# A two-layer recurrent trunk: beta and decay columns in fp32 strips, other order at the beginning, for low parts, state update and output factor

## The chip, the cores and the metric

The kernel runs on one core of a Trainium2 chip. The metric is the device time of one execution in microseconds (us), the median of several runs. The core's engines work side by side: TensorE (PE) multiplies matrices into PSUM, VectorE (DVE) and ScalarE (ACT) work elementwise, GpSimd (POOL) does small element work and issues some transfers, SyncE (SP) issues the weight transfers.

## What is computed

The reference is a decoder trunk of two layers over 256 prompt tokens and 8 x 8 sample tokens, 320 tokens in all, with a width of 1024. Each layer is a half-step feed-forward block (SwiGLU, 2816 wide), a mixer, and another half-step feed-forward block, each with an RMS norm before and after; a last norm follows. The mixer reads one input projection:

```python
proj = h @ w_in     # [rg_x | q | k | v | rg_gate | z | beta_logit | decay_logit]
conv_out, new_buf = causal_conv(proj[..., :CONV_CH], conv_buf, conv_w)   # width 4, on rg_x, q, k, v
beta = sigmoid(scal[..., :DN_HEADS])
g = -exp(dn_a_log) * softplus(scal[..., DN_HEADS:] + dn_dt_bias)
o, S = gated_delta(q, k, v, g, beta, S0)
o = rmsnorm(o, dn_norm_w) * silu(z)
```

One half of its width is a gated linear recurrence (`rg_lru`), the other a gated delta rule with four heads of 128, computed in chunks of 64 tokens with a triangular solve per chunk. Beta and decay are the last 8 of 3080 columns of `w_in`. The final states are outputs too.

## The kernel before

Activations are kept transposed, features on the partitions and 320 tokens along the free dimension. A product in fp32 accuracy is made of three fp32r products: a weight block of 128 columns is loaded by SP as `raw` (L122), ScalarE rounds it to its high part `wh` (L130), VectorE subtracts to get the low part `wl` (L135), and `Unit.mm` (L158) issues `xh*wh`, `xh*wl` and `xl*wh` for each of 8 blocks of the contraction, 24 matmuls a unit. There are five raw buffers, and three pairs for wh and wl beside two larger spare ones.

PE's order is written out by hand, the other engines' order is laid out by the compiler from priorities: `tc.high_priority(offset=n)` puts instructions ahead as if they had been written n places earlier. A `Fill` object holds a stage's units; `F(n)` issues the next n of their matmuls, `F.to(i)` all up to unit i, and the small matmuls of the mixer are put between such calls, so that the fills cover the waits of the small work. The lists FL, FZ and FY (L60) hold these n.

At the boundary to the mixer (`boundary`, L404) the residual is updated block by block, and `F.inter` issues three matmuls of each of the first four units for every block: the 8-column unit of beta and decay and the first three of k. Its PSUM tile is scaled in `scal_done` (L710), transposed at L760 into token order, and VectorE makes beta and g of it in a row of small operations (L765 to L773, softplus at L264 to L276). The units of k, q, v, rg, z and gate follow; each finished unit of the first four kinds goes through `conv` (L662: L674, L675, three L686, an activation at L707). g is summed by the matmuls from L796 on, decay differences are made at L828, k*k at L892, the solve runs from L914 on, and q*k at L936 needs all four q heads. The recurrence's gates (L1070) and scan (`rg_scan`, L1073) run beside it.

At the end, two blocks p of sample states are updated: four matmuls each (L1212, 32 rows by 512 columns), four additions into the state (L1216), two transfers out. `scale_o` (L1047) multiplies the outputs by a root factor, made on POOL by a power (L1052), and `finish_o` transposes them (L1225).

The program begins (L1296 on) with the loads of x and of the first three weight units in halves, dummy matmuls on a tile of ones (L1330), transposes of x (L1335, L1336), and the first 72 matmuls. Then come the sums of squares (L1412) and the first row factor rsb (L1421, L1422).

## Time and profile before

| | us |
|---|---|
| median of 3 runs (1279.4 to 1281.31) | 1279.9 |
| the profiled execution | 1281.22 |
| its span | 1279.3 |
| PE busy | 1250.1 |
| VectorE busy | 853.2 |
| ScalarE busy | 698.1 |
| GpSimd busy | 109.3 |

The span runs from the first to the last instruction; what the execution takes beyond it lies around it. PE busy is the union of its matmul durations, which overlap, so a busy PE need not be at its peak. The granted clock is TensorE's, 1.00 for full speed. Times in the rows count from the start of the span; the mixers of the two layers stand at about 256 to 395 and 880 to 1017 us.

### The profile page before, as it was taken

The page shows a single profiled execution, that of the slowest core. Times are in us where ns is not written, and L with a number is a line of the kernel's source. Part 1 is how long each engine was busy: PE and PEld are TensorE (multiplying, and loading weights), DVE is VectorE, ACT ScalarE, POOL GpSimd, SP SyncE. Part 2 cuts the span into 40 slices and gives each one's busy share as a digit, 9 for nine tenths or more (in the row PEclk, how much of TensorE's full clock was granted, in tenths as well). Part 3 has the DMA queues.
Part 4 walks back from the last instruction along what each step waited for, and adds up shares of the span by engine and source line. Part 5 has one row for each costly group of instructions (what it writes and reads, how often), then busy time and mean ns, then how long its engine had stood idle before and what let it go on. Part 6 is the DMA issues. An engine that isn't in the chain of part 4 may idle for free.

```text
span 1279.3 us, 24478 instructions
## 1 busy us (share of the span) xinstructions
PE 1250.1 (98%) x9812; PEld 1216.5 (95%) x9812; DVE 853.2 (67%) x1541; ACT 698.1 (55%) x1220; POOL 109.3 (9%) x241
## 2 busy tenths in 40 slices
PE   9999999998999999999999999999899999999996
PEld 7999999998979999999999999999899899999995
DVE  4976644799776866654486665459986877666444
ACT  5654444675686644444464444446749675444443
POOL 1100000232130100000000000013411210000000
PEclk9999999998989999999999999999999899999998
DMA  8555555563346455555645555575332655555551
GB/s 207 156 171 161 161 152 167 137 159 84 84 131 174 118 165 160 161 152 168 181 118 159 162 165 153 164 193 141 89 84 59 186 152 166 164 165 156 147 143 42
DMA packets 356470, 187.26 MB, mean 146 GB/s; under 512 B 9034, under 2 KB 353436, under 8 KB 356356
## 3 DMA queue, kind: packets, MB, share of 16 engines
q1 hardware_dynamic: 353124, 178.12, 49.3%
q0 software_dynamic: 2672, 6.65, 1.9%
q8 instruction: 77, 1.26, 0.4%
q10 hardware_dynamic: 560, 0.93, 0.2%
q14 instruction: 37, 0.30, 0.1%
HBM read 179.16 MB, written 6.51 MB: 145 GB/s over the span
## 4 chain that ended last, share of the span: by engine, by line
PE 90%; DVE 6%; ACT 2%; DMA 1%; issue 1%; POOL 0%; SPq 0%; DVEq 0%; ACTq 0%
PE mm L158 44%; PE sm L158 38%; PE sm L914 2%; PE st L231 1%; DMA raw<-in_ffn_w_up_dram 1%; PE sm L978 1%; DVE co L686 1%; DVE wl L135 1%; DVE xr L1094 1%; DVE aux L1216 0%; PE sm L936 0%; DVE nA L921 0%; DVE DN L828 0%; PE sm L1070 0%; DVE bt L425 0%
## 5 line engine op out<-in xcount | busy, mean ns | idle before, releaser
L135 DVE TENSOR_TENSOR wl<-raw,wh 128x1024 fp32r<-128x1024 f32 x321 | 384.4, 1198 | 214.1 <-ACT wh L130 209.8
L130 ACT ACTIVATE wh<-raw 128x1024 fp32r<-128x1024 f32 (+1 forms) x316 | 326.6, 1036 | 367.5 <-issue 127.0
L158 PE MATMUL mm<-xh,wl 128*128 128x320 f32 x976 | 294.8, 306 | 7.8 <-DVE wl L135 7.8
L158 PE MATMUL mm<-xh,wh 128*128 128x320 f32 x976 | 295.6, 308 | 1.0 <-ACT wh L1352 0.8
L158 PE MATMUL mm<-xl,wh 128*128 128x320 f32 x976 | 287.8, 305 | 0.0
L158 PE MATMUL sm<-xh,wh 128*128 128x320 f32 x720 | 215.6, 299 | 0.0
L158 PE MATMUL sm<-xl,wh 128*128 128x320 f32 x720 | 215.5, 299 | 0.0
L158 PE MATMUL sm<-xh,wl 128*128 128x320 f32 x720 | 215.4, 299 | 0.0
L158 PEld LDWEIGHTS mm<-xh,wl 128*128 128x128 f32 x976 | 186.2, 192 | 12.9 <-DVE wl L135 8.7
L158 PEld LDWEIGHTS mm<-xh,wh 128*128 128x128 f32 x976 | 186.7, 192 | 6.0 <-issue 1.5
L158 PEld LDWEIGHTS mm<-xl,wh 128*128 128x128 f32 x976 | 183.8, 192 | 2.7 <-issue 1.1
L158 PEld LDWEIGHTS sm<-xh,wl 128*128 128x128 f32 x720 | 136.1, 189 | 0.3 <-DVE wl L135 0.3
L158 PEld LDWEIGHTS sm<-xh,wh 128*128 128x128 f32 x720 | 136.1, 189 | 0.0
L158 PEld LDWEIGHTS sm<-xl,wh 128*128 128x128 f32 x720 | 136.1, 189 | 0.0
L158 PE MATMUL sm<-gh,wh 128*128 128x320 f32 x374 | 112.2, 300 | 0.0
L158 PE MATMUL sm<-gh,wl 128*128 128x320 f32 x374 | 111.8, 299 | 0.0
L158 PE MATMUL sm<-gl,wh 128*128 128x320 f32 x374 | 111.8, 299 | 0.0
L158 PE MATMUL mm<-gh,wh 128*128 128x320 f32 x330 | 99.0, 300 | 0.0
L158 PE MATMUL mm<-gh,wl 128*128 128x320 f32 x330 | 98.7, 299 | 0.0
L158 PE MATMUL mm<-gl,wh 128*128 128x320 f32 x330 | 98.7, 299 | 0.0
L158 PEld LDWEIGHTS sm<-gh,wl 128*128 128x128 f32 x374 | 70.7, 189 | 0.0
L158 PEld LDWEIGHTS sm<-gh,wh 128*128 128x128 f32 x374 | 70.7, 189 | 0.0
(438 smaller groups left out, 1966.3 us busy)
## 6 DMA issues: line engine op xcount, KB each, us to landing
raw<-in_ffn_w_up_dram SPq DMA_DIRECT2D x173, 512.0 KB, 3.8
raw<-in_ffn_w_down_dram SPq DMA_DIRECT2D x64, 512.0 KB, 3.9
raw<-in_w_in_dram SPq DMA_DIRECT2D x48, 512.0 KB, 4.0
raw<-in_ffn_w_down_dram SPq DMA_DIRECT2D x32, 384.0 KB, 3.4
raw<-in_w_out_dram SPq DMA_DIRECT2D x16, 512.0 KB, 3.9
aux<-in_state_delta_dram SPq DMA_DIRECT2D x8, 512.0 KB, 7.5
out_dram<-aux POOLq DMA_DIRECT2D x8, 512.0 KB, 5.3
raw<-in_ffn_w_up_dram SPq DMA_DIRECT2D x6, 256.0 KB, 7.5
```

The costliest lines, as they stand in the source:

```text
L130: act(wh[:, :nk], raw[:, :nk], *((AF.Copy,) if tok is None or tok[0] else (AF.Identity, tok[1]())))
L135: (sub or dve).tensor_sub(wl[:, :nk], raw[:, :nk], wh[:, :nk].bitcast(F32))
L158: pe.matmul(self.blk.ps(), w, il(xx), start=self.first and self.pos == 1, stop=self.last and self.pos == 3 * self.nk)
L231: pe.matmul(ps[:, t:t + 1], s[:, a:b], ones[:, 0:1], start=start and t == 0, stop=stop, skip_group_check=True)
L686: stt(co, cb[:, w:w + CVW], cwc(w), co, op0=OP.mult, op1=OP.add)
L914: pe.matmul(ps[HF[h], 64 * i:64 * i + 64], lhs(u, h), rhs(u, h), start=True, stop=True)
L978: pe.matmul(ps[32 * j:32 * j + 32, 128 * i:128 * i + 128], kz[:, h, i, c:c + 32], SS[p][:, j // 2, 4 * (j % 2) + b], start=b == 0, stop=b ...
L1094: dve.tensor_tensor_scan(xr[:, c], aa[:, c], it[:, c], 0.0, op0=OP.mult, op1=OP.add)
```

## The change

The unit of beta and decay goes. In its place `ws` holds the 64 fp32 columns, multiplied by the norm's gain and padded, and after the boundary's blocks 3 and 7 four fp32 matmuls each take 32 columns of it (8 of them a block's own) into four 32-partition strips of one PSUM tile; a selection matrix `sel8` adds the strips when they are brought into token order. All following unit numbers fall by one, k has all four units in `inter`, and the fill lists change. The low parts of `w_in` get a priority offset of 100. Each state update issues two matmuls, fills, and two more. The output factor of all but the first group is made by Sqrt on ScalarE and a reciprocal. At the beginning the x loads change queue and order, dummies are added, and the prefetch calls move between the sums of squares.

```diff
+HPL = 100
-FL = [14, 37, 32, 9, 15, 8, 0, 14, 0, 11, 10, 8, 6, 4, 4, 6, 21, 1, 8, 0, 16, 6, 11]
+FL = [6, 33, 28, 9, 15, 8, 0, 10, 0, 11, 10, 8, 6, 4, 4, 6, 20, 1, 8, 0, 8, 16, 11]
...
-            (sub or dve).tensor_sub(wl[:, :nk], raw[:, :nk], wh[:, :nk].bitcast(F32))
+            with tc.high_priority(offset=hp):
+                (sub or dve).tensor_sub(wl[:, :nk], raw[:, :nk], wh[:, :nk].bitcast(F32))
...
+        sel8 = C["sel8"] = consts.tile([128, 8], F32, name="sel8")
+        dve.tensor_add(sel8, ident[:, 0:8], ident[:, 32:40])
+        dve.tensor_add(sel8, sel8, ident[:, 64:72])
+        dve.tensor_add(sel8, sel8, ident[:, 96:104])
...
             F.inter(n, 1)
+            if hook:
+                hook(k)
...
-            act(wsh, wsr, AF.Copy)
-            dve.tensor_sub(wsl, wsr, wsh.bitcast(F32))
-            units = [Unit(lambda a: (wsh, wsl), Blk(smtile, 8), xsplit, done=lambda ps: self.scal_done(ps))]
+            pool.memset(ws[:, 8:11], 0.0)
+            dve.tensor_mul(ws[:, 0:8], wsr, C["vec"][:, 0, g0:g0 + 8].unsqueeze(2).to_broadcast([128, 8, 8]))
...
+        def scal(self, k):
+            if k % 4 < 3:
+                return
+            if k == 3:
+                self.scps = smtile()
+            for j in range(4):
+                i = k - 3 + j
+                w = self.ws.rearrange("p k c -> p (k c)")[:, 8 * i:8 * i + 32]
+                pe.matmul(self.scps[32 * j:32 * j + 32, :T], w, x[:, i], start=k == 3, stop=k == 7)
...
-                pe.transpose(tp[:, t * 8:(t + 1) * 8], self.sc8[:, t * 128:(t + 1) * 128], ident[0:8, 0:8])
+                pe.matmul(tp[:, t * 8:(t + 1) * 8], self.sc8[:, t * 128:(t + 1) * 128], C["sel8"], start=True, stop=True)
...
-                pool.tensor_tensor(fs[:, us], fs[:, us], mhalf[:, us], op=OP.pow)
+                if u0:
+                    act(fs[:, us], fs[:, us], AF.Sqrt, bias=self.tok_s)
+                    dve.reciprocal(fs[:, us], fs[:, us])
+                else:
+                    pool.tensor_tensor(fs[:, us], fs[:, us], mhalf[:, us], op=OP.pow)
...
-                F(FL[19 + p])
-                ps2 = [smtile() for _ in range(4)]
-                for j in range(4):
...
                 for h in range(2):
+                    F(FL[19 + p] if h == 0 else 6)
+                    ps2 = [smtile() for _ in range(2)]
+                    for j in range(2):
+                        r = slice(64 * h + 32 * j, 64 * h + 32 * j + 32)
+                        pe.matmul(ps2[j], kd[r, u], ve[r], start=True, stop=True)
...
+        nc.sync.dma_start(xtok[0:64, 2, c], x_sample.rearrange("b s d -> (b s) d")[:, c])
         nc.sync.dma_start(xtok[:, 0, c], x_prompt[0, 0:128, c])
         nc.sync.dma_start(xtok[:, 1, c], x_prompt[0, 128:256, c])
-        nc.scalar.dma_start(xtok[0:64, 2, c], x_sample.rearrange("b s d -> (b s) d")[:, c])
...
         pt = [xin(j) for j in range(4)]
+        dummies(6)
...
-            mm4(0)
+            for j in range(4):
+                F.u[0].mm()
+                if hf == 0:
+                    dummies((2, 3, 2, 0)[j])
...
-                pt = [xin(4), xin(5)]
+                dummies(5)
+                pt = [xin(4)]
+                dummies(2)
+                pt += [xin(5), xin(6), xin(7)]
...
-                pt += [xin(6), xin(7)]
...
-        F.prefetch(5)
...
         for t, r in enumerate((128, 128, 64)):
+            F.prefetch(4 + min(t, 1))
             act(hpf[0:r, :D], xtok[0:r, t], AF.Square, accum_out=ss[0:r, t:t + 1])
```

## Rows read from the trace of the kernel before

**Rows 1.** The page, busy time of the engines: us (share of the span) xinstructions
```profile
PE 1250.1 (98%) x9812; PEld 1216.5 (95%) x9812; DVE 853.2 (67%) x1541; ACT 698.1 (55%) x1220; POOL 109.3 (9%) x241
```

**Rows 2.** The chain that ended last, in order: start us, us, what
```profile
258.13 0.28 PE sm L760 x3
...
268.89 0.22 PE sm L797 x2
...
344.09 1.08 PE sm L1070 x4
...
445.47 9.78 PE mm L158 x72
```

**Rows 3.** Groups by line: line, engine, operation, xcount | busy us, mean ns | idle before
```profile
L135 DVE TENSOR_TENSOR wl<-raw,wh 128x1024 fp32r<-128x1024 f32 x321 | 384.4, 1198 | 214.1 <-ACT wh L130 209.8
...
L158 PE MATMUL sm<-xh,wsh 128*8 128x320 f32 x16 | 4.8, 300 | 0.2
```

**Rows 4.** Waits of PE, the longest: us in total, times, longest us
```profile
PE mm L158 <- DVE wl L135: 7.8, 4, 3.5
```

**Rows 5.** Windows: us, busy per engine (xinstructions), granted clock, DMA share, GB/s
```profile
288.00:292.00 4.00, 0.68 (x7) 0.43 (x3) 4.00 (x8) 3.79 (x9) 1.79 (x4) 0.92 0.00 0
292.00:296.00 4.00, 3.85 (x15) 3.65 (x15) 4.00 (x12) 2.17 (x7) 2.29 (x5) 0.50 0.59 149
...
374.00:378.00 4.00, 2.52 (x11) 2.12 (x10) 3.82 (x7) 3.57 (x7) 2.57 (x4) 0.50 1.01 254
```

**Rows 6.** Timeline of PE, first layer's solve: start us, us, what [idle before]
```profile
307.48 1.08 PE L978 MATMUL sm<-aux,hp 128*32 128x128 f32 x32
308.49 0.40 PE L158 MATMUL mm<-xh,wl 128*128 128x320 f32 x1
308.73 0.30 PE L158 MATMUL mm<-xl,wh 128*128 128x320 f32 x1
```

**Rows 7.** Timeline of DVE, first layer's mixer
```profile
267.11 0.15 DVE L276 TENSOR_TENSOR sv<-sp,nal 128x10 f32<-128x10 f32 x1
...
281.59 1.38 DVE L921 SCALAR_TENSOR_TENSOR nA<-sm,sv,DN 128x128 f32<-128x128 f32 x5 [0.38 <-PE sm L892]
...
287.50 3.46 DVE L686 SCALAR_TENSOR_TENSOR co<-cb,vec,co 128x344 f32<-128x344 f32 x7
290.87 1.22 DVE L135 TENSOR_TENSOR wl<-raw,wh 128x1024 fp32r<-128x1024 f32 x1
```

**Rows 8.** Timeline of PE, the end of that stretch
```profile
292.14 0.64 PE L158 MATMUL mm<-xh,wl 128*128 128x320 f32 x1 [3.46 <-DVE wl L135]
...
294.17 1.91 PE L936 MATMUL sm<-qa,ka 128*128 128x128 f32 x8
```

**Rows 9.** Timeline of ACT, first layer's mixer
```profile
283.48 2.10 ACT L130 ACTIVATE wh<-raw 128x1024 fp32r<-128x1024 f32 x2
...
292.61 0.51 ACT L707 ACTIVATE qa<-co,tok 128x256 f32<-128x256 f32 x1
```

**Rows 10.** Timeline of PE, end of the first layer's mixer
```profile
369.24 1.86 PE L1212 MATMUL sm<-at,kd 32*128 32x512 f32 x4 [0.35 <-DVE hp L1091]
...
376.08 1.11 PE L1225 MATMUL sm<-ident,qa 128*128 128x128 f32 x4 [1.48 <-DVE aux L1216]
```

**Rows 11.** Timeline of DVE, the same stretch
```profile
369.24 0.68 DVE L1216 TENSOR_TENSOR aux<-aux,sm 128x512 f32<-128x512 f32 x1
...
370.57 1.26 DVE L1216 TENSOR_TENSOR aux<-aux,sm 128x512 f32<-128x512 f32 x2
...
375.34 2.48 DVE L1216 TENSOR_TENSOR aux<-aux,sm 128x512 f32<-128x512 f32 x4
```

**Rows 12.** Timeline of ACT, the same stretch
```profile
374.40 0.69 ACT L1057 ACTIVATE qa<-qa,fs 128x128 f32<-128x128 f32 x2 [2.65 <-POOL fs L1052]
```

**Rows 13.** Timeline of PE, the beginning
```profile
15.29 2.50 PE L158 MATMUL mm<-xh,wh 128*128 128x320 f32 x8
...
34.72 0.60 PE L1421 MATMUL sm<-ident,rs 128*128 128x128 f32 x3 [1.57 <-DVE rs L237]
```

More of the change, by code (lines that the diff above doesn't have):

```diff
@@ L402, in build_consts, with boundary @@
         yield late
[L404 removed]
+    def boundary(slast, gname, l, F, n, side, ahead=0, hook=None):
         side = list(side) + [None] * 3
@@ L1207, in run @@
                 ve = ves[p]
[L1208 to L1217 removed]
+                for h in range(2):
+                    F(FL[19 + p] if h == 0 else 6)
[3 more added lines that the diff above has]
+                        pe.matmul(ps2[j], kd[r, u], ve[r], start=True, stop=True)
+                    for j in range(2):
+                        sv4 = S[:, h, 4 * j:4 * j + 4].rearrange("p b e -> p (b e)")
+                        with tc.high_priority(offset=HPO):
+                            dve.tensor_add(sv4, sv4, ps2[j])
                     nc.gpsimd.dma_start(dn_s[l][:, 2 * p + h].rearrange("b d e -> d b e"), S[:, h])
@@ L1325, in trunk @@
     gp0 = ph.fp.tile([128, 16], F32, name="gp0", bufs=1)
+    dps = []
     def dummies(m):
-        ps = sttile()
+        dps[:] = dps or [sttile()]
         for _ in range(m):
-            pe.matmul(ps[:, :T], ph.gh[:, 0, :128], ph.gh[:, 0], start=True, stop=True)
+            pe.matmul(dps[0][:, :T], ph.gh[:, 0, :128], ph.gh[:, 0], start=True, stop=True)
     def xin(k):
```

52 lines of the change are left out of this document (25 added, 27 removed).

## The prediction

> **What bounds the kernel now.** I read the page first: TensorE (PE) is busy for 98% of the span [rows 1], so time can only come from matmuls that go, from the few stretches in which PE waits, and from stretches in which it runs slowly. The chain gives the unit of account: 72 fill matmuls in 9.78 us, 0.136 us each [rows 2]; mean durations of about 300 ns in the groups are latencies, not spacing. The 8-column unit of beta and decay pays the same price as a full unit: 300 ns mean, with 24 matmuls a layer [rows 3]. The waits of PE then name the largest loss: four waits on low-part subtractions (wl, L135), 7.8 us [rows 4], the layers repeating each other. The windows show a second loss behind such a wait: PE busy for 0.68 of 4 us, then a granted clock of 0.50, which is the 1.2 GHz level, while it works on; at the end of the mixer it is 0.50 again [rows 5].
>
> **The change part by part.** Times are of the first layer; each stands twice unless said.
>
> *Beta and decay.* Removed: 24 matmuls, 24 x 0.136 = 3.26 us. Added: two groups of four fp32 strips over 320 columns. No row has this shape. The nearest: 16 fp32 matmuls of 32 columns by 128, in four strips, take 1.01 us from their start to the next matmul [rows 6]; full-width fp32 matmuls over 320 columns take 1.08/2 = 0.54 us each [rows 2]. At 128 columns that is 0.22 us, so 16 in series would be 3.5 us and the strips overlap 3.5-fold. A group is then 0.54 x 4 / 3.5 = 0.62 us; the ends are 0.54 (full overlap) and 2.16 (none). The matmul after such a group starts 0.24 instead of 0.136 us before its successor [rows 6], so leaving the strips costs 0.10. Two groups: 1.45 us, bounds 1.1 to 4.5. The Trainium skill's TensorE: Matmul & The Clock Gate (Part 3) measures 2.38-fold for three column tiles; by that the sum would be 0.2 us worse for both layers together. The skill's TensorEngine Tiling (Key Properties) says that a mode switch drains the array, which speaks against short groups; the 0.10 us above is what it costs in this trace.
>
> The three transposes (0.28 us) become three fp32 matmuls with full weights, 0.22 each by a row of that kind [rows 2]: +0.38. With 6 instead of 14 fills in front, PE reaches them about 0.4 us before sc8 is scaled. Net on PE: 3.26 - 1.45 - 0.38 - 0.4 = 1.0 us. But g, which the next sums need, is ready at 267.1 [rows 7], right before PE reads it; the strips put it 1.2 us later, so PE reaches those sums at the old time, only 8 fills further on (the change takes 16 fills out in front). The gain must survive the next stretch.
>
> *Low parts.* PE stands still from 288.7 to 292.1 for one wl [rows 8]. VectorE (DVE) is the limit there: seven conversions (3.46 us) stand ahead of that wl [rows 7], though its wh was made by 285.6 [rows 9]. Raising wl by 100 puts it first. What is late next: the conversions themselves. qk waits for all four q heads, and the last is activated at 292.61 [rows 9], ready at 293.0. DVE has the same work to do up to there whichever order it takes, and begins 1.2 us later. So qk, now at 294.17 [rows 8], comes between 293.0 (DVE makes up its start from its own idle time) and 295.4 (the next wl, 1.14 us, is put ahead too); I take 294.0. PE is then 4 fills further (0.54 us) and waits for qa instead of wl, with the low clock as before. Gain 0.6 us a layer, bounds -0.7 to +1.7.
>
> *State update in pairs.* Now: four row strips, then 16 fills, then four that must wait for PSUM banks which DVE's additions free. The second four begin at 369.24 and the output transposes at 376.08, after another 1.48 us of waiting [rows 10], since DVE ends the first half's additions at 371.8 and starts the second half's at 375.34 [rows 11]. The clock is at its low level around there [rows 5]. After: 2, 6 fills, 2, 8 fills, 2, 6 fills, 2, 16 fills. A strip's 512 fp32 columns take 512/320 x 0.54 = 0.86 us, whether one or three others run beside it, so a pair costs as much as four did; with a switch, 0.95 us, and four groups in place of two, 1.9 us more PE time. From 365.2: first pair to 366.2, second to 368.1, third from 369.9 (its banks free at 369.84 [rows 11], 0.6 us of waiting) to 370.9, fourth from 371.9 to 372.9, transposes at 375.1 instead of 376.08. If DVE keeps the additions at 375.34, it is 376.1. PE has then done 14 fills more (1.9 us), without a gap of the kind that now goes ahead of the low clock; that lasts about as long as one window of 4 us, in which PE does half of what it could, 1.9 us lost. Gain 1.9 + 1.9 + (0 to 1.0): I take 4.0 a layer. If the clock falls all the same, 1.9.
>
> *Output factor.* POOL's power becomes a Sqrt and a reciprocal. ScalarE now waits 2.65 us for POOL there [rows 12], but the transposes behind it wait for DVE, not for that. I cost it at nothing: 0.2 to 0.3 us on each of two engines, hidden behind 16 fills (2.2 us); uncovered, at most 0.5 a factor. The Sqrt is ordered after the scan's Sqrt by a token, so it needs no table of its own.
>
> *Beginning* (once). PE waits 1.57 us for rsb at 34.72 [rows 13], because the sums of squares wait for a memset that stands behind two wl on DVE; it now comes ahead of both, so the first square starts earlier: 1.57 us go. The two moved loads go from ScalarE's queue to SP's, and what follows them there is issued that much later; I cost it at nothing while PE waits for x anyway, and leave it to the bounds. The dummies: eight matmuls at 15.29 take 2.50 us [rows 13], twice the later spacing, so PE still runs slowly, in a stretch full of gaps. If the new dummies bring full pace at about 14 us, the 36 matmuls of the first half gain what the 20 dummies (2.7 to 5.3 us) cost. Taken: -0.3, bounds -2.5 and +1.8. Together 1.3 us.
>
> *Edits taken at nothing:* the gain in ws and the selection matrix, four small operations under VectorE's 214 us of waiting for ScalarE [rows 3]; the layer's first load is read by a product that also needs the vectors, and both are done long before the mixer. POOL loses two power operations and gains one small memset, nothing that PE waits for.
>
> **Sum:** 2 x 0.6 + 2 x 4.0 + 1.3 = 10.5 us. The profiled execution took 1281.2 us (span 1279.3), so 1270.7 there; it stands 1.3 us over the median of the runs, which puts the median at 1279.9 - 10.5 = 1269.4.
>
> **The rivals.**
> *The early stall goes altogether:* the conversions are done sooner because DVE finds them ready, and qk finds qa. For: the wait is only one subtraction long. Against: DVE is busy 4.00 of 4 us there [rows 5]. It returns 3.5 us and some 2 us of low clock per layer, 10 more in all: 1259.4.
> *The late stall stays:* DVE's additions keep their place, PE waits at the transposes, the clock falls. Late gain 1.9 a layer: 1273.6.
> *The strips don't overlap* (each strip then pays its full 0.54 us): 2 x 3.1 us more: 1275.6. Rows 6 speak against it.
> *No rise of the clock at the beginning:* PE is still slow at 15.29, after dummies and transposes [rows 13], and stays so until the first half is done. The 20 dummies then cost about 2.5 us where -0.3 was taken: 1271.6. The Trainium skill's TensorE: Matmul & The Clock Gate (Part 4) says that transposes don't count as activity for the clock, which would make this more likely; no row here shows it apart.
> *Slower:* a raised wl at the head of DVE's in-order queue whose wh is not yet made. DVE's wait for wh is already 209.8 us in all [rows 3], harmless elsewhere. Ahead of the solve, ScalarE makes two wh only from 283.5 to 285.6 [rows 9]; a wl placed before the chain that begins at 281.59 [rows 7] holds it for some 3.3 us, the next ones for 1.0 and 1.7, with the conversions behind: 6 us a layer, against the 0.6 gained. At the end of the mixer two more hold the additions by some 2 us each layer. Sum: 10.5 - 13.2 - 4 = 6.7 slower, 1286.6. It decides from about 6.5 us of such standing a layer; below, the kernel is only less fast.
>
> **How the numbers follow.** 0.2% is 2.6 us, about what a measurement can tell here from no change. Chances: forecast 0.47, late stall 0.20, early stall gone 0.15, no rise at the beginning 0.08, serial strips 0.04, held queue 0.03, the fills only move and nothing is gained (1279.9) 0.03. The range takes in the early stall gone and serial strips: 1258 to 1276. Faster 0.91: all but the last two, less part of their edges; same 0.05, slower 0.04.
>
> **What would show it.** Right: no wait of PE on wl in the mixers, but one on qa of some 4 us at qk; two groups of four strips with the next matmul 0.6 to 0.7 us behind; no granted clock of 0.50 at the mixer's end, transposes about 1 us earlier there and 14 fills more done; no wait at rsb, which comes 1 to 3 us sooner. Wrong: idle VectorE in front of wl in the mixers; strips 0.5 us apart; additions after wl at the mixer's end; a wait of more than 1 us at the sc8 matmuls.

## The result, and the profile after

The changed kernel takes 1300.2 us (median of 4 runs), the one before 1280.6 us beside it: 1.0153 times as long, 95% interval 1.0140 to 1.0166. I had forecast 1269.4 us, with 0.04 for any slowdown. The profiled execution has a span of 1298.2 us, 18.9 more than the one before.

**Where the 18.9 us are.** The two layers have the same stages, and each mixer begins and ends with the same six-column sums. Both traces, timeline of PE (start us, us, engine, line, operation); first the kernel before, at the start and the end of its two mixers:

```profile
235.10 0.72 PE L231 MATMUL st<-ones,acc 128*128 128x1 f32 x6
416.20 0.73 PE L231 MATMUL st<-ones,acc 128*128 128x1 f32 x6
859.10 0.72 PE L231 MATMUL st<-ones,acc 128*128 128x1 f32 x6
1038.19 0.73 PE L231 MATMUL st<-ones,acc 128*128 128x1 f32 x6
```

and the changed kernel at three of these places (the fourth is at 1056.86):

```profile
234.48 0.72 PE L233 MATMUL st<-ones,acc 128*128 128x1 f32 x6
425.41 0.73 PE L233 MATMUL st<-ones,acc 128*128 128x1 f32 x6
868.29 0.72 PE L233 MATMUL st<-ones,acc 128*128 128x1 f32 x6
```

The mixers took 181.10 and 179.09 us and now take 190.93 and 188.57: 9.8 and 9.5 us more. Everything ahead of the first is 0.6 us shorter, the rest is within 0.3 us of what it was. So the whole loss is in the two mixers. In the first layer the state update, which stood 130.28 us behind the mixer's first sums, stands at 136.64; from there to the end it took 50.82 and now takes 54.29. 6.4 us are lost ahead of the state update, 3.5 us behind it. The two lines (timeline of PE), before and after:

```profile
365.38 1.14 PE L1212 MATMUL sm<-nA,kd 32*128 32x512 f32 x8
```

```profile
371.12 1.13 PE L1240 MATMUL sm<-nA,kd 32*128 32x512 f32 x4
```

**The waits of PE in the changed kernel** (us in total, times, longest us), against the single long wait on wl of [rows 4]:

```profile
PE mm L160 <- DVE wl L137: 7.8, 4, 3.5
PE mm L160 <- ACT kd L1256: 4.9, 2, 2.5
PE mm L160 <- DVE cb L684: 4.2, 2, 2.1
PE sm L816 <- ACT co L693: 3.2, 2, 1.9
PE mm L160 <- ACT vo L1260: 2.3, 2, 1.1
```

The wait that the raise was to remove is still there at its old length (L137 is the old L135), and four others have come: for the g sums (L816), for a PSUM tile (cb), and at the end of the mixer for the finished outputs (kd, vo). At L816 the profile names an operation of ScalarE; that one and g end within 0.05 us of each other, just ahead of the sums.

**Windows of the changed kernel** (from, to and length in us; busy time of PE, PEld, DVE, ACT and POOL with instructions; granted clock; DMA share; GB/s):

```profile
268.00:272.00 4.00, 2.13 (x17) 1.92 (x15) 3.49 (x12) 3.65 (x7) 2.76 (x6) 0.94 0.87 221
272.00:276.00 4.00, 4.00 (x22) 4.00 (x22) 1.79 (x7) 0.15 (x1) 0.19 (x1) 0.63 0.53 131
...
280.00:284.00 4.00, 2.85 (x14) 2.60 (x15) 2.05 (x9) 3.97 (x16) 1.52 (x7) 0.72 0.01 2
...
292.00:296.00 4.00, 1.10 (x9) 0.85 (x7) 3.95 (x12) 2.40 (x4) 0.00 (x0) 0.93 0.00 0
296.00:300.00 4.00, 3.43 (x43) 3.03 (x44) 4.00 (x7) 1.64 (x5) 0.41 (x2) 0.50 0.52 139
...
392.00:396.00 4.00, 1.15 (x3) 0.58 (x3) 3.95 (x8) 3.99 (x9) 0.00 (x0) 0.80 0.46 131
396.00:400.00 4.00, 3.61 (x13) 3.61 (x14) 3.48 (x7) 2.30 (x4) 0.00 (x0) 0.50 0.48 139
```

[Rows 5] show one such pair of windows early and one late. Now there are three early ones: PE stands still, and the clock is then lower (0.63, 0.72, 0.50) while it works on. The late one has moved from 374 to 396 us and is as deep as before.

**What stands ahead of g.** Timeline of DVE in the changed kernel, the lines that answer to [rows 7]:

```profile
258.05 0.49 DVE L732 TENSOR_TENSOR PY<-sm,rsb 128x320 f32<-128x320 f32 x1 [1.16 <-ACT rsb L448]
...
264.35 1.22 DVE L137 TENSOR_TENSOR wl<-raw,wh 128x1024 fp32r<-128x1024 f32 x1
...
266.13 1.22 DVE L137 TENSOR_TENSOR wl<-raw,wh 128x1024 fp32r<-128x1024 f32 x1
...
270.19 0.17 DVE L278 TENSOR_TENSOR sv<-sp,nal 128x10 f32<-128x10 f32 x1
```

Two raised wl of 1.22 us stand inside the softplus row, none of them with idle time ahead of it: g is made at 270.19 instead of 267.11. The chain also begins later: beta and decay are scaled at 23.57 us behind the mixer's first sums instead of 21.75.

**What that does to ScalarE.** The same stretch, timeline of ACT; first the last activation of k in the kernel before, where the Exp follows at 274.44, then the changed kernel:

```profile
271.52 0.40 ACT L707 ACTIVATE ka<-co 128x256 f32<-128x256 f32 x1
```

```profile
270.87 1.28 ACT L858 ACT_TABLE_LOAD   x1
277.06 0.63 ACT L858 ACTIVATE DN<-DN 128x512 f32<-128x512 f32 x1 [4.90 <-DVE DN L848]
...
280.68 1.28 ACT L716 ACT_TABLE_LOAD   x1
281.97 0.42 ACT L716 ACTIVATE ka<-co 128x256 f32<-128x256 f32 x1
```

The Exp of the decay differences and its table load now stand ahead of the last k head's activation (ka). ScalarE waits 4.90 us for DN with that ka queued behind it, has to go back to the other table (1.28 us), and makes at 281.97 what the kernel before had made before its Exp. The transposes of k (L877), k*k and the solve wait for it.

### The profile page after: what moved, and what is told of

Its sections match the earlier page's. It is cut to its first block, busy times and chain, and to the rows that moved or that the text cites. A ratio compares the mean times of both kernels' runs of the same rounds, so it can differ in the third digit from the quotient of the medians.

```text
span 1298.2 us, 24498 instructions
## 1 busy us (share of the span) xinstructions
PE 1256.8 (97%) x9822; PEld 1223.0 (94%) x9822; DVE 854.3 (66%) x1550; ACT 697.0 (54%) x1222; POOL 91.9 (7%) x239
## 4 chain that ended last, share of the span: by engine, by line
PE 88%; DVE 7%; ACT 3%; issue 1%; DMA 0%; POOL 0%; SPq 0%; DVEq 0%
PE mm L160 42%; PE sm L160 36%; PE sm L934 2%; PE st L233 1%; DVE wl L137 1%; PE sm L1240 1%; DVE co L695 1%; PE sm L998 1%; ACT qa L1081 0%; ACT wh L131 0%; DMA xtok<-in_x_prompt_dram 0%; PE st L1359 0%; PE sm L877 0%; DVE nA L941 0%; PE sm L1094 0%
## 5 line engine op out<-in xcount | busy, mean ns | idle before, releaser
L137 DVE TENSOR_TENSOR wl<-raw,wh 128x1024 fp32r<-128x1024 f32 x321 | 384.0, 1197 | 214.2 <-ACT wh L131 209.9
L160 PE MATMUL mm<-xh,wh 128*128 128x320 f32 x960 | 290.9, 307 | 4.5 <-DVE cb L684 4.2
L160 PE MATMUL mm<-xh,wl 128*128 128x320 f32 x960 | 288.4, 305 | 7.0 <-DVE wl L137 7.0
L160 PE MATMUL mm<-xl,wh 128*128 128x320 f32 x960 | 284.5, 306 | 0.2
L160 PE MATMUL sm<-xh,wl 128*128 128x320 f32 x736 | 220.5, 300 | 0.1
L160 PE MATMUL sm<-xh,wh 128*128 128x320 f32 x736 | 220.6, 300 | 0.0
L160 PE MATMUL sm<-xl,wh 128*128 128x320 f32 x736 | 220.3, 299 | 0.0
L160 PEld LDWEIGHTS mm<-xh,wh 128*128 128x128 f32 x960 | 183.2, 192 | 12.4 <-DVE cb L684 4.7
L160 PEld LDWEIGHTS mm<-xh,wl 128*128 128x128 f32 x960 | 183.1, 192 | 8.5 <-DVE wl L137 7.4
L160 PEld LDWEIGHTS sm<-xh,wl 128*128 128x128 f32 x736 | 139.1, 189 | 0.3 <-DVE wl L137 0.3
L160 PEld LDWEIGHTS sm<-xl,wh 128*128 128x128 f32 x736 | 139.1, 189 | 0.0
```

The costliest lines, as they stand in the source:

```text
L137: (sub or dve).tensor_sub(wl[:, :nk], raw[:, :nk], wh[:, :nk].bitcast(F32))
L160: pe.matmul(self.blk.ps(), w, il(xx), start=self.first and self.pos == 1, stop=self.last and self.pos == 3 * self.nk)
```

## The experiments

Runs are named by the first part of their labels. "Mixers" is the time between those sums, first and second layer, in the run's profile; "update" is the first state update of the first layer, counted from the first sums. Each median stands against the kernel before on the same chip (1279.7 to 1280.6 us).

| run | edit | median us | ratio to before (95%) | mixers | update |
|---|---|---|---|---|---|
| before | | 1280.6 | 1 | 181.1, 179.1 | 130.3 |
| after | all | 1300.2 | 1.0153 (1.0140 to 1.0166) | 190.9, 188.6 | 136.6 |
| e1 | after, wl not raised | 1295.3 | 1.0119 (1.0102 to 1.0135) | 187.2, 187.2 | 136.0 |
| e2 | after, factor on GpSimd | 1305.0 | 1.0192 (1.0175 to 1.0210) | 192.4, 190.3 | 135.2 |
| e3 | after, four updates at once | 1305.3 | 1.0202 (1.0183 to 1.0221) | 191.0, 193.0 | 136.7 |
| e4 | before, wl raised | 1291.9 | 1.0101 (1.0079 to 1.0123) | 187.3, 187.2 | 136.1 |
| e5 | before, pairs, factor, beginning | 1281.5 | 1.0009 (0.9999 to 1.0019) | 180.0, 179.0 | 130.3 |
| e6 | before, strips | 1293.1 | 1.0104 (1.0085 to 1.0122) | 187.5, 185.4 | 136.4 |
| e7 | e1, 16 dummies | 1292.1 | 1.0091 (1.0076 to 1.0107) | 192.6, 179.2 | 138.4 |
| e8 | before, pairs | 1278.3 | 0.9990 (0.9980 to 0.9999) | 178.4, 178.3 | 128.9 |
| e9 | e1, five fills later | 1296.8 | 1.0124 (1.0110 to 1.0137) | 187.0, 187.3 | 135.7 |
| e10 | e8, one wl raised | 1276.8 | 0.9966 (0.9956 to 0.9977) | 178.2, 178.2 | 128.7 |
| e11 | e8, that wl on GpSimd | 1280.7 | 1.0002 (0.9994 to 1.0011) | 178.4, 179.5 | 129.0 |
| e12 | e9, that wl on GpSimd | 1291.0 | 1.0081 (1.0068 to 1.0095) | 184.7, 184.4 | 133.5 |
| e13 | e6, strips behind the sums | 1291.7 | 1.0096 (1.0076 to 1.0116) | 187.0, 182.9 | 135.9 |
| e14 | before, beginning | 1281.8 | 1.0011 (1.0002 to 1.0020) | 179.0, 180.8 | 128.9 |
| e15 | before, factor | 1282.1 | 1.0010 (1.0001 to 1.0019) | 179.6, 181.2 | 129.1 |
| e16 | e13, pairs, one wl raised | 1286.0 | 1.0043 (1.0030 to 1.0057) | 182.3, 181.9 | 132.7 |
| e17 | e13, row factor ahead of fills | 1290.8 | 1.0088 (1.0072 to 1.0105) | 184.5, 184.3 | 133.4 |
| e18 | e17, pairs, one wl raised | 1284.7 | 1.0032 (1.0018 to 1.0047) | 181.5, 181.6 | 132.0 |

Mixers of kernels whose mixers differ from the one before in nothing or little (before, e14) lie between 179.0 and 181.1 us, so 2 us in one mixer of one profile prove nothing; the medians and the waits do.

### The raised low parts: e1 and e4

```diff
-HPL = 100
+HPL = 0
```

> Edit: the changed kernel with the priority offset of wl set from 100 to 0. The changed kernel reaches its first state update 6.4 us later per layer than the kernel before, counted from the sums of squares at the mixer's boundary (136.6 against 130.3 us), although it has 24 fill matmuls fewer behind it. Theory A, the raised wl stand ahead of softplus and conversions on VectorE, and the last k head's activation falls behind the Exp on ScalarE: without the raise, all four activations of ka come ahead of the Exp's table load, PE's waits of 1.9 us at the g sums and 2.1 us for cb go, the state update is reached at 128 to 131 us from the boundary, and the time falls by 2 x 5.5 to 2 x 8: 1284 to 1289. Rival B, the strips and the four k units that now finish together do it, whatever wl's place: 1297 to 1300.

```diff
-            (sub or dve).tensor_sub(wl[:, :nk], raw[:, :nk], wh[:, :nk].bitcast(F32))
+            with tc.high_priority(offset=hp):
+                (sub or dve).tensor_sub(wl[:, :nk], raw[:, :nk], wh[:, :nk].bitcast(F32))
...
-                    units.append(Unit(lambda a, c=base + 128 * h: wload(w_in[l], 0, 8, c, a, tok=(False, xtoken) if c == 512 else None), Blk(smtile if base + h == 1027 else mmtile), xsplit,
+                    units.append(Unit(lambda a, c=base + 128 * h: wload(w_in[l], 0, 8, c, a, tok=(False, xtoken) if c == 512 else None, hp=HPL), Blk(smtile if base + h == 1027 else mmtile), xsplit,
```

> Edit: the kernel before, with only the low parts of w_in raised by 100. Theory A (raised wl delay the conversions and what follows): its wait of 3.5 us on wl goes, but the solve starts 2 to 6 us later per layer: 1283 to 1292. Rival B (the raise is harmless or good, the rest of the change does the damage): 1272 to 1280.

In the kernel before, the raise alone costs 12.1 us: theory A, as far as that kernel goes. (The profiled execution took 1296.7 us, the slowest of four, so its stretches show the loss at its largest.) Its trace shows the same first step, timeline of DVE:

```profile
267.04 1.21 DVE L137 TENSOR_TENSOR wl<-raw,wh 128x1024 fp32r<-128x1024 f32 x1
268.17 0.16 DVE L278 TENSOR_TENSOR sv<-sp,nal 128x10 f32<-128x10 f32 x1
```

Such a wl is put right ahead of the last operation of g. PE waits for g and then for a PSUM tile, and what follows is in the windows of e4:

```profile
268.00:272.00 4.00, 2.62 (x18) 2.32 (x18) 2.56 (x10) 1.50 (x4) 0.90 (x5) 0.83 0.79 196
272.00:276.00 4.00, 4.00 (x20) 4.00 (x19) 2.61 (x7) 1.77 (x3) 1.19 (x2) 0.50 0.50 138
```

At the low clock the decay sums (L822), for which DN and ScalarE wait, take 3.62 us; at the full clock, in the kernel before, they took 1.95. Two waits of 0.36 and 1.02 us have become a delay of the chain: k*k comes at 49.42 us behind the first sums instead of 45.39. Later, raised wl stand between the conversions of the q heads, and PE, which waited 3.5 us once for wl, now waits three times for qa, 4.6 us in all (timeline of PE in e4):

```profile
294.00 0.49 PE L938 MATMUL sm<-qa,ka 128*128 128x128 f32 x2 [0.47 <-ACT qa L709]
296.11 0.49 PE L938 MATMUL sm<-qa,ka 128*128 128x128 f32 x2 [1.62 <-ACT qa L709]
299.13 0.80 PE L938 MATMUL sm<-qa,ka 128*128 128x128 f32 x2 [2.53 <-ACT qa L709]
```

In the changed kernel, taking the raise away gave back only 5.0 us, and not where theory A said: all four activations of ka come ahead of the Exp again and the late stretch shrinks from 54.3 to 51.2 us, but the state update is still at 136.0. So rival B is right for the early part of the changed kernel: something beside the raise holds it up.

### The late part: e2, e3 and e8

```diff
-                if u0:
-                    act(fs[:, us], fs[:, us], AF.Sqrt, bias=self.tok_s)
-                    dve.reciprocal(fs[:, us], fs[:, us])
-                else:
-                    pool.tensor_tensor(fs[:, us], fs[:, us], mhalf[:, us], op=OP.pow)
+                pool.tensor_tensor(fs[:, us], fs[:, us], mhalf[:, us], op=OP.pow)
```

> Edit: the changed kernel with all output factors made by GpSimd's power again. From the first state update to the sums of squares behind the mixer the changed kernel takes 54.3 us where the one before took 50.8, and ScalarE waits 5.9 us for fs (L1071) with the last qa, the Sigmoid-side table load and kd behind that wait. Theory C, the Sqrt in ScalarE's queue holds the output: kd comes 3.5 to 5 us earlier against the state update, PE's waits for kd and vo (2.5 and 1.1 us) go, 1290 to 1293. Rival D, the 14 fills that the pairs use up are missing at kd whoever makes the factor: the wait stays over 2 us, 1298 to 1300.

```diff
-                    F(FL[19 + p] if h == 0 else 6)
-                    ps2 = [smtile() for _ in range(2)]
+                F(FL[19 + p])
+                ps2 = [smtile() for _ in range(4)]
...
```

> Edit: the changed kernel with four state-update matmuls at once and the fill counts of the kernel before there (0, 16, 6). Theory C (the factor's place holds the output): the 14 fills go back behind the transposes and cover some of the wait for kd, but the waits at the second four and at the transposes return; nothing gained or 1 us per layer lost: 1299 to 1303. Rival D (the pairs used up the fills that covered kd): the late part gets back its 3.5 us per layer: 1292 to 1294.

Both made the changed kernel 5 us slower, outside what either theory gave. The Sqrt does hold ScalarE (it waits 5.94 us for fs in the changed kernel), but on GpSimd the late stretch is 57.2 us instead of 54.3, and with four updates at once the old waits come back (0.61 and 1.19 us in the first layer). Neither edit by itself is the late loss. In e1 it goes with the raise (51.2 us), but the raise alone has 51.2 too (e4), and e7 below has 54.2 in its first layer without any raise: what sets the late loss off is not shown.

The pairs by themselves, in the kernel before (the change's edit of the state update with its fill counts, and nothing else):

```diff
-                F(FL[19 + p])
-                ps2 = [smtile() for _ in range(4)]
...
+                    F(FL[19 + p] if h == 0 else 6)
+                    ps2 = [smtile() for _ in range(2)]
...
```

> Edit: the kernel before with the state update in pairs and its fill counts; the factor stays on GpSimd. My sum for the late part had 4.0 us a layer: 1272. If only the wait at the transposes goes and the low clock stays, 1276. If the fills that are used up are missing later and PE waits for kd, 1279 to 1283. In the changed kernel, pairs with the factor on GpSimd had waits of 0.7 us on qa at the transposes and 1.3 to 2 us on wh and wl behind them, so a result at the middle of these is the likeliest.

1278.3: a gain of 0.1%, by its interval between 0.1 and 2.6 us, where my late term was 8.0. (The profiled execution, 1276.1 us, is the fastest of ten.) PE waits 0.47 us at the fourth pair, where I had 0.6 at the third, and not at the transposes, and no clock of 0.50 follows. With 36 fills in place of 22 (14 x 0.136 = 1.9 us more) the stretch from the state update to the transposes is 11.13 us instead of 10.70: the transposes come 0.4 us later, where I had up to 1.0 earlier, and the gain up to them is 1.5. From them to the first product of the finished outputs it takes 9.27 us instead of 13.16; less the 14 fills that is another 2.0, about what I had for the clock. But the fills done ahead are missing afterwards. PE reaches that product at 149.3 instead of 154.1 us, and there it waits (timeline of PE in e8, first layer):

```profile
383.96 0.37 PE L158 MATMUL mm<-kd,wh 128*128 128x320 f32 x1 [0.59 <-DVE bt L735]
385.04 0.40 PE L158 MATMUL mm<-kd,wl 128*128 128x320 f32 x1 [0.71 <-DVE wl L135]
```

From that product to the mixer's end it takes 29.05 us instead of 26.96: 2.1 us are given back. In the changed kernel PE waits at the same place of the first layer for kd (2.46 us), vo (1.14) and a wl (0.43), 4.0 us in all, and the window behind it is at 0.50. That this is the same lack of fills is not shown: e3, which moves the 14 fills back, has a late stretch of 54.2 us all the same.

### The strips: e5, e6, e7, e9, e13 and e17

e5 is the kernel before with the change's edits of the state update, the factor and the beginning, without the strips and the raise. e6 has the strips, their fill counts and the unit numbers; with these one q unit's PSUM tile comes from the small pool and the first prefetch is four units instead of five, as in the changed kernel, and what these two do alone was not tried:

```diff
+            if hook:
+                hook(k)
...
-            units = [Unit(lambda a: (wsh, wsl), Blk(smtile, 8), xsplit, done=lambda ps: self.scal_done(ps))]
...
```

> Edit: the kernel before with the new beginning, the state update in pairs and the new output factor; no strips and no raised wl. Theory E (what costs in the changed kernel beside the raise is that the cheap unit of beta and decay is gone: PE reaches the next low parts and the g sums 16 to 24 fills sooner, on a VectorE that is busy all the time, stands still and falls to the low clock): the early mixer is as before (solve and state update at 130 us from the boundary), the late part gains 2 to 4 us a layer, the beginning 0.7: 1271 to 1276. Rival F (pairs or factor cost by themselves, the strips do not): 1284 to 1290.

> Edit: the kernel before with the strips for beta and decay, the unit taken out and the early fill counts cut with it; nothing else. Theory E: a new wait of PE of 2 to 3 us for a wl or for g at 36 us from the boundary, with the low clock behind it, 5 to 8 us a layer: 1290 to 1296. Rival F: the two groups take 2 x 0.7 us in place of 3.3 and the layer gains 1 us or loses nothing: 1277 to 1281.

Without the strips (and the raise) the time is within 0.2% of the kernel before, outside what either theory gave for e5: the early mixer is as before, as theory E has it, but the late gain is not there. With the strips alone the time is 13.4 us above. So the strips' edit brings the early loss. Not by their own price: a group takes 0.68 us to the next matmul (246.10 to 246.78 in the changed kernel), as costed. The wl in question in the kernel before, and then the strips-alone run, timeline of DVE and then of PE:

```profile
267.68 1.23 DVE L135 TENSOR_TENSOR wl<-raw,wh 128x1024 fp32r<-128x1024 f32 x1
```

```profile
257.45 0.49 DVE L730 TENSOR_TENSOR PY<-sm,rsb 128x320 f32<-128x320 f32 x1 [0.68 <-ACT rsb L446]
...
268.83 1.22 DVE L135 TENSOR_TENSOR wl<-raw,wh 128x1024 fp32r<-128x1024 f32 x1
```

```profile
270.10 0.40 PE L158 MATMUL mm<-xh,wl 128*128 128x320 f32 x1 [2.61 <-DVE wl L135]
```

Count from the mixer's first sums (233.98 here, 235.10 before). The sums of squares at the boundary's end stand 1.74 us later (19.67 instead of 17.93), because the two strip groups come on top there: the fourth k unit has taken the place of the unit of beta and decay. With them comes the row factor, and VectorE's scaling moves from 21.75 to 23.47. The wl of the fourth unit after k is ready at 36.07 instead of 33.81, 2.26 later; 1.72 of it are the later start, and the rest is order (three units' cb now stand ahead of the first conversion, so VectorE's order is not quite the same, as the expectation of e13 has it). PE needs it for the 74th fill of these units, and reaches that fill at 33.5 instead of 35.39, 1.9 earlier: the fourth k unit's fills and the g sums no longer stand ahead of it. In the kernel before the wl was 1.58 us early. 2.26 + 1.9 - 1.58 = 2.6: the new wait. Behind it (windows of e6):

```profile
268.00:272.00 4.00, 1.90 (x14) 1.90 (x14) 3.02 (x7) 1.96 (x4) 1.54 (x5) 0.92 0.18 38
272.00:276.00 4.00, 4.00 (x17) 4.00 (x18) 2.96 (x8) 1.76 (x5) 1.64 (x4) 0.50 0.33 97
276.00:280.00 4.00, 4.00 (x27) 4.00 (x26) 2.52 (x10) 1.75 (x3) 0.00 (x0) 0.73 0.49 131
```

PE is busy all the time there at half and three quarters of the clock, and what it does are fills, the g sums and the decay sums. VectorE waits for these sums and is busy for only 2.96 and 2.52 of 4 us. The delay feeds itself.

```diff
             F(FL[0])
...
+            dum(8)
...
             F(FL[1])
+            dum(4)
...
             F(FL[2])
+            dum(4)
```

> Edit: the run with wl not raised, and 16 dummy matmuls of a fill's size put where the unit's fills were taken out: 8 before the transposes of beta and decay, 4 and 4 before the g sums. They compute nothing. Theory E, with the clock as the dearer half: the 2.2 us of dummies take the place of the 2.6 us wait on wl at 36 us from the boundary, the clock of 0.50 in the 5 us behind it stays at 1.00, and 2 to 3 us a layer come back although PE does more: 1288 to 1292, against 1295.3 without them. Rival G (the wait costs only its own length, or VectorE is simply later): 1294 to 1300.

The dummies compute nothing and add 2.2 us of work to each layer. In the second layer the mixer falls from 187.2 to 179.2 us, 8 us, although PE does more: it still waits 0.89 and 0.79 us, but the granted clock is 1.00 from 890 to 938 us, and the state update comes at 127.9, sooner than in the kernel before (129.0). In the first layer the wait stays (2.78), and the mixer grows to 192.6. The layers differ in VectorE's queue: with the same code, that wl stands ahead of g in the second layer, ready at 33.0 us, and behind g in the first, ready at 37.5 (35.9 and 36.1 in e1). So the second layer owes the missing wait to VectorE's order and not to the dummies; its scaling is as late as in e6 (23.46), and the loss is gone all the same. The median lies at the edge of what theory E gave, and the run does not show its mechanism.

```diff
-FL = [6, 33, 28, 9, 15, 8, 0, 10, 0, 11, 10, 8, 6, 4, 4, 6, 20, 1, 8, 0, 8, 16, 11]
+FL = [6, 33, 23, 14, 15, 8, 0, 10, 0, 11, 10, 8, 6, 4, 4, 6, 20, 1, 8, 0, 8, 16, 11]
```

> Edit: the run with wl not raised, with five fills moved from ahead of the g sums to behind them (fill counts 28, 9 become 23, 14). Counted over the units that follow the four k units, the g sums stand behind fill 69 in the kernel before and behind fill 77 in the changed one; fill 74 is the first that needs the fourth wl, which VectorE makes only after g. Theory E2: what the strips broke is this order, PE waits for that wl ahead of the g sums where it used to come behind them. With the five fills behind, the wait of 2.6 us becomes at most 1 us on g, the clock of 0.50 behind it goes, and 2 to 4 us a layer come back: 1287 to 1291. Rival H (the four k units' conversions, all due at once, keep VectorE back, and the order of the fills changes nothing): the wait only changes its name, 1293 to 1297.

The forecast of theory E2 failed: the wait follows the fills (2.31 us behind the g sums, and 1.07 ahead of them), and the time does not fall. But VectorE makes that wl later too (ready at 38.5 us instead of 36.1), so the edit moved two things, and what the order of the fills does alone is not shown.

```diff
-            if hook:
-                hook(k)
...
+        if hook:
+            hook(3)
+            hook(7)
```

> Edit: the run with the strips alone, both groups moved from between the boundary's blocks to right behind its sums of squares. In the strips-alone run these sums stand at 19.7 us from the boundary instead of 17.9; the row factor, and with it VectorE's whole chain, starts 1.7 us later, the fourth wl is ready at 36.1 instead of 33.8 us, and PE, which is there at 33.5 us, waits 2.6. VectorE's order is the same in both runs. Theory S (the late start): the wait falls to 0.8 to 1.2 us, and 1.7 us of delay, with some of the low clock, come back per layer: 1285 to 1290, against 1293.1. Rival H (the four k units' conversions bunched on VectorE): the wait stays above 2 us and the time above 1291.

Inconclusive: ten fills stand between the sums and the row factor's matmul on PE, and I had put the strips ahead of these. The scaling came at 23.0, only 0.4 us earlier, and the wait stayed at 2.62. Wait and time lie where rival H put them, but the late start that theory S wanted away was still there.

```diff
-        F(10)
+        F(1 if hook else 10)
...
-FL = [6, 33, 28, 9, 15, 8, 0, 10, 0, 11, 10, 8, 6, 4, 4, 6, 20, 1, 8, 0, 16, 6, 11]
+FL = [15, 33, 28, 9, 15, 8, 0, 10, 0, 11, 10, 8, 6, 4, 4, 6, 20, 1, 8, 0, 16, 6, 11]
```

> Edit: the run with the strips behind the sums of squares, with nine of the ten fills between these sums and the row factor's matmul moved behind that matmul. The scaling of beta and decay should start at 21.8 to 22.2 us from the boundary, as in the kernel before (21.75), instead of 23.0. Theory S (the late start of VectorE's chain): the fourth wl is ready at 33.8 to 34.5 us, PE reaches it at 33.1 to 33.5 and waits at most 1.2 us instead of 2.6, the clock stays, and 3 to 5 us a layer come back: 1282 to 1287, against 1291.7. Rival H (the conversions of four k units come at once, and VectorE's order, not its start, is the cause): the wait for the wl or for g stays above 2 us, 1289 to 1294.

Now the scaling is at 21.86, and the wait is gone: PE waits 0.28 us at the g sums and comes to the decay sums at 36.05 us, as before (36.07). But this is not theory S as forecast. The wl is ready at 31.5 us and not at 33.8 to 34.5, because VectorE's order has changed with the fills. Timeline of DVE, e13 and then e17:

```profile
268.00 0.15 DVE L276 TENSOR_TENSOR sv<-sp,nal 128x10 f32<-128x10 f32 x1
...
268.70 1.22 DVE L135 TENSOR_TENSOR wl<-raw,wh 128x1024 fp32r<-128x1024 f32 x1
```

```profile
264.57 1.21 DVE L135 TENSOR_TENSOR wl<-raw,wh 128x1024 fp32r<-128x1024 f32 x1
...
267.42 0.15 DVE L276 TENSOR_TENSOR sv<-sp,nal 128x10 f32<-128x10 f32 x1
```

In e13 it stands behind g, in e17 ahead of it, in both layers. The edit moved start and order together, and the time, 1290.8 us, is in the range of rival H. Little came back: 2.4 us against the strips-alone run by the medians (3.0 us in the first mixer, 1.1 in the second). PE now waits further on (timeline of PE in e17, its waits):

```profile
275.61 0.40 PE L158 MATMUL mm<-xh,wh 128*128 128x320 f32 x1 [1.56 <-DVE cb L683]
277.31 0.43 PE L158 MATMUL mm<-xh,wl 128*128 128x320 f32 x1 [1.30 <-DVE wl L135]
...
294.17 0.40 PE L158 MATMUL mm<-xh,wl 128*128 128x320 f32 x1 [4.94 <-DVE wl L135]
```

The same v unit for which PE waited 3.46 us [rows 8] now costs 4.94, and the one two units ahead of it, which cost 0.42, costs 2.86 together with its PSUM tile. What the runs show together: where that wl stands behind g (e1, e6, e13, e9, e7's first layer), PE waits 2.3 to 2.8 us for it; where it stands ahead of g (e17, e7's second layer), PE does not, whether the chain starts at 21.86 or at 23.46 us. So VectorE's order, together with how early PE comes, decides on the first wait; that the later start alone makes it is not shown. And with this wait gone the mixers of e17 are still 3.4 and 5.2 us longer than before, by waits for VectorE further on; in e7's second layer, where dummies keep PE busy for 2.2 us, they are short. That fits work taken from PE coming back as waits for VectorE, but the two runs differ in more than that.

### The two small terms: e14 and e15

e14 has the change's edits of the beginning alone, e15 those of the factor alone:

```diff
+            F.prefetch(4 + min(t, 1))
...
```

```diff
+                if u0:
+                    act(fs[:, us], fs[:, us], AF.Sqrt, bias=self.tok_s)
...
```

> Edit: the kernel before with the new beginning alone. My sum had -1.3 us: 1278.5. The profiles so far put the row factor's matmul at 33.1 to 34.7 us in four runs with the old beginning and at 32.5 to 35.2 us in six with the new one, so what they say is no gain: 1279 to 1281. The run with pairs, factor and beginning had new waits on wl between 40 and 60 us that cost 2.9 us: if they belong to the beginning, 1282 to 1283.

> Edit: the kernel before with the new output factor alone. My sum had 0: 1280. The stretch from the state update to the end of the mixer took 49.7 and 49.9 us with pairs, factor and beginning against 49.4 with pairs alone, which makes the factor 0.3 to 0.5 us dearer per layer: 1280 to 1282. If the 5 us that it gives in the changed kernel is its own, 1275 to 1278.

Both are 0.1% slower, 1.5 and 1.8 us, with intervals that just leave out no change. In e14 the row factor's matmul is at 32.6 us instead of 34.7, earlier as forecast; but the prefetches that moved between the squares change VectorE's order, and three new waits on wl between 44 and 60 us take 2.4 us (0.95, 1.02 and 0.41; the longest, timeline of PE in e14):

```profile
55.74 0.40 PE L158 MATMUL sm<-xh,wl 128*128 128x320 f32 x1 [1.02 <-DVE wl L135]
```

The changed kernel does not have these waits, and gained 0.6 us there. The factor's price of 0 was near, and its sign depends on what is beside it: 1.8 us dearer here, 4.8 cheaper in e2.

### The one wl, and versions: e10, e11, e12, e16 and e18

```diff
-                    units.append(Unit(lambda a, c=base + 128 * h: wload(w_in[l], 0, 8, c, a, tok=(False, xtoken) if c == 512 else None), Blk(smtile if base + h == 1027 else mmtile), xsplit,
+                    units.append(Unit(lambda a, c=base + 128 * h: wload(w_in[l], 0, 8, c, a, tok=(False, xtoken) if c == 512 else None, hp=100 if c == 1792 else 0), Blk(smtile if base + h == 1027 else mmtile), xsplit,
```

> Edit: the run with pairs alone, and only the one wl raised by 100 for which PE stands 3.5 us (the third v unit). This is the early term of my sum by itself: that wl comes ahead of seven conversions, PE goes on 4 fills further and then waits for qa; 0.6 us a layer, bounds -0.7 to +1.7: 1275 to 1280, against 1278.3 for the pairs alone. If the raise itself were harmful wherever it is put, 1283 and more.

```diff
-                    units.append(Unit(lambda a, c=base + 128 * h: wload(w_in[l], 0, 8, c, a, tok=(False, xtoken) if c == 512 else None), Blk(smtile if base + h == 1027 else mmtile), xsplit,
+                    units.append(Unit(lambda a, c=base + 128 * h: wload(w_in[l], 0, 8, c, a, tok=(False, xtoken) if c == 512 else None, sub=pool if c == 1792 else None), Blk(smtile if base + h == 1027 else mmtile), xsplit,
```

> Edit: the run with pairs alone, and that one wl made by GpSimd instead of VectorE. If VectorE's time is what bounds this stretch, 1.2 us are taken from it, and PE waits neither for this wl nor 3.5 us for qa: 2 to 4 us a layer with the clock, 1270 to 1275. If GpSimd needs more than 3 us for it or keeps VectorE waiting, nothing: 1277 to 1281.

e12 makes this edit in e9's kernel.

> Edit: the run with five fills later, and the wl of the third v unit made by GpSimd. If both stalls of the early mixer go, the changed kernel without the raise gains 2 to 4 us a layer on top of that run: 1280 to 1285. If the late loss of the changed kernel (54.3 against 50.8 us from the state update on) is still there, it stays above the kernel before.

e10 is my early term by itself, and the queues went as worked out: the wl at 288.22 comes ahead of seven conversions, nothing else in VectorE's order ahead of it moves, qk is reached at 54.67 instead of 59.06 us, and PE waits for qa instead (timeline of PE in e10):

```profile
292.15 0.49 PE L937 MATMUL sm<-qa,ka 128*128 128x128 f32 x2 [1.25 <-ACT qa L708]
...
294.23 0.60 PE L937 MATMUL sm<-qa,ka 128*128 128x128 f32 x2 [0.91 <-ACT qa L708]
```

The state update gains 0.2 us a layer in the profile, where I had 0.6. The medians of e10 and e8, each against the kernel before in its own comparison, differ by 0.24%, some 3 us. The traces do not show where the rest of that comes from (the profiled execution of e8 is the fastest of its ten, that of e10 the slowest of its eight), so the size of this gain is not explained. At 1276.8 us, 0.9966 times the kernel before (0.9956 to 0.9977), e10 beats both kernels.

On GpSimd the same wl gained nothing (e11), and the trace shows why. It takes GpSimd 2.36 us, and the pair of copies that VectorE has then takes 2.71 us instead of 0.90 (timelines of POOL and of DVE in e11):

```profile
284.89 2.36 POOL L135 TENSOR_TENSOR wl<-raw,wh 128x1024 fp32r<-128x1024 f32 x1 [1.96 <-ACT wh L130]
```

```profile
285.28 2.71 DVE L925 COPY_PREDICATED Nt<-mN,nA 64x256 f32<-64x256 int32 x2
```

VectorE was spared 1.2 us and held for 1.8, in both layers: the second branch of the expectation. In e12 a conversion of 0.57 us takes 2.68 in the same way, beside a wl of 2.35 us on GpSimd. So e11 does not tell whether VectorE's time bounds that stretch. e12 is 5.8 us below e9, within the 2 to 4 us a layer that I expected of GpSimd's wl there, but e9 had not fallen, so 1291.0 lies above the range; it is 4.3 us below e1.

e16 is e13 and e18 is e17, each with e8's and e10's edits.

> Edit: strips behind the sums of squares, the state update in pairs, and the one wl of the third v unit raised. If the gains add (pairs 1.3, the one wl 1.5) to what the strips cost behind the sums: about 3 us under that run, 1282 to 1287, and still above 1276.8, the best so far.

> Edit: the same with the state update in pairs and the wl of the third v unit raised. Theory S: 3 to 5 us a layer under the run with strips behind the sums, pairs and that wl (1286.0): 1276 to 1280, as good as the best run without strips (1276.8). Rival H: 1284 to 1287.

e16 came out where it was expected; e18's 1284.7 lies in the range of rival H and not at the 1276 to 1280 of theory S. With pairs and the one wl, the strips cost 8 to 9 us against e10 in both. I found no place at which they pay; a version with less work on VectorE beside them was not tried.

## Why the prediction was wrong

- **What bounds the kernel** was read right as far as it went: PE, except where it waits for VectorE. But the sum treated PE's and VectorE's times as if one could be shortened under the other. In the early mixer, where VectorE sets the pace, work taken from PE was worth nothing in these runs.
- **Beta and decay.** The price of the groups was right: four strips in 0.68 us where one full-width matmul takes 0.54 [rows 2], 3.2-fold. The Trainium skill's TensorE: Matmul & The Clock Gate (Part 3) has 2.38-fold for three tiles; for four, this trace decides. The serial rival is out. The step that failed is "PE reaches those sums at the old time, only 8 fills further on". It missed that the strips stand ahead of the sums of squares, so that VectorE's whole chain starts 1.7 us later and g comes 2.1 us later (I had 1.2), and that the 8 fills cross into the next unit, whose wl is made only behind g: in e6 the wait of 2.6 us and the low clock behind it. 13.4 us for the kernel where the sum had nothing of its own. How much of this the start, the missing work on PE and VectorE's order each bring stays open: every edit that moved one of them moved VectorE's order too.
- **Low parts.** "Raising wl by 100 puts it first" holds for one wl, raised alone (e10). The raise is on all units of w_in, and "DVE has the same work to do up to there whichever order it takes" is wrong: the order decides whether g and the conversions, which PE, ScalarE and the solve wait for, come ahead of 1.2 us pieces that nobody needs yet. 12.1 us instead of -1.2. The rival of a held queue had the sign, and with 6.7 us slower the size of a good half; its mechanism was another. VectorE did not stand waiting for wh: such waits come to 25.0 us in the two mixers of the kernel before (235 to 425 and 860 to 1060 us), to 23.4 in e4 and 23.6 in the changed kernel. Each wl's own time was the delay, and in the changed kernel ScalarE's order (Exp ahead of ka) followed; with the raise alone (e4) it did not. I gave it 0.03, because I asked whether wl would block and not what it would displace.
- **State update in pairs.** The clock and the 14 fills came as forecast, the transposes 0.4 us later instead of up to 1.0 earlier; the failed step is the sum "1.9 + 1.9 + (0 to 1.0)", which ends at the transposes. Fills are moved, not saved: a layer has as many, and those spent ahead are missing where the outputs are finished (2.1 us in the first layer of e8). By the medians a layer gains 0.7 us, not 4.0.
- **Output factor and beginning:** priced 0 and -1.3, measured +1.8 and +1.5 alone. The rival of no rise of the clock is out: in the changed kernel five dummies at 15.71 us take 0.89 us, the full pace, which came at 18.5 before. The mechanism at rsb was right and was given back by wl that I had not asked about: moving the prefetch calls moves conversions of weights, which the text costed at nothing. In the changed kernel the wait at rsb is gone, but rsb comes only 0.7 us sooner; there PE also waits 1.67 us for x (1.3 in e14, not at all before), the term of the moved loads that I had put at nothing.
- **The parts do not add.** Against the kernel before, raise, strips, pairs, factor and beginning alone are +12.1, +13.4, -1.3, +1.8 and +1.5, 27.5 us in all; together they are 19.6. Raise and strips both make PE wait for VectorE in the same stretch, and the wait is paid once (state update of the first layer at 136.1, 136.4 and with both 136.6).

## What to carry to other kernels

Before work is taken from the engine that is busy all the time, look in each stretch for the engine that delivers to it: if that one is busy all the time too, the saved work comes back as a wait, and the wait as a lower clock. A priority raised for a whole class of instructions must be costed by what it displaces on an in-order queue, not by what it brings forward; raise the one instruction that is waited for. Filler work is a stock: where it is spent earlier, ask what it had covered. And where a compiler orders the other engines' queues, an edit of one queue moves the others: look up where the instruction that was waited for now stands before a theory gets the credit.

## What was not expected of the hardware

One and the same wait is not always followed by a lower clock. At the boundary between the two layers PE waits 0.6 us for the row factor in both of these profiles. Kernel before, and then e5, whose code is the same there (windows, columns as above):

```profile
640.00:644.00 4.00, 3.90 (x28) 3.51 (x27) 3.63 (x9) 1.81 (x4) 0.00 (x0) 1.00 0.67 179
```

```profile
640.00:644.00 4.00, 4.00 (x19) 4.00 (x18) 3.93 (x10) 2.25 (x5) 0.00 (x0) 0.57 0.42 118
```

The stage that holds it took 221.46 us in the one and 222.60 in the other. In e7's second layer two waits of 0.89 and 0.79 us left the clock at 1.00. A single profile therefore says little about an edit worth 1 us; what decided here was repeated medians and the place of the waits.
